# A squared-ReLU MLP in seven products per pair: feature pairs worked on two at a time, and operand reloads issued ahead and split over the products

## The chip, the cores and the metric

The kernel runs on one core of a Trainium2 chip. The metric is the device time of one execution in microseconds (us); the median of the runs is compared.

## What is computed

One layer of a diffusion backbone over 1024 tokens of width 1024, in fp32. The part around the change is the MLP at its end:

```python
def sq_relu_mlp(h, w1, w2):
    return jnp.square(jax.nn.relu(h @ w1.astype(jnp.float32))) @ w2.astype(jnp.float32)
...
hm = modulate(rmsnorm(xs_, pre_mlp_g[i]), sh2, sc2)
xs_ = xs_ + g2 * rmsnorm(sq_relu_mlp(hm, w_mlp1[i], w_mlp2[i]), post_mlp_g[i])
```

`h` is 1024 x 1024, `w1` is 1024 x 4096, `w2` is 4096 x 1024.

## The kernel before

Each matmul operand is held as two fp32r parts, a high half (a copy on ACT) and a low half (a difference on DVE). A product of two such operands takes three matmuls for each 128 rows of the contraction.

Both layers of the MLP are computed with a Strassen-Winograd scheme: a 2 x 2 block product in seven block products instead of eight. A "pair" is two feature tiles of 128, one from either half, and both token blocks of 512. For each pair there are seven products, in the order 1, 2, 6, 5, 7, 3, 4 (`ORDER`, line 1155). A product (`mm_op`, line 1217) is 12 matmuls of 128 x 128 by 128 x 512. Three PSUM banks hold the seven: bank x takes products 1, 6, 7 and 4 one upon the other, bank y takes 5 and 3, bank v takes 2. Between two products on a bank, `evac` reads the bank: in layer one with a copy (`snap`, on ACT) or a sum (on DVE) into `stage`, then ReLU and square on ACT; in layer two into `acc`, copies on ACT for the first chunk and sums on DVE after it.

There are 27 pairs. Layer one has 13 in this form (`S1`), after three done as plain products; each ends with four sums (`finish`) and a write of `stage` to `hid_d` in DRAM, from the POOL queue. Layer two has 14 (`S2`): four chunks of the hidden features, four pairs each, less two that the final stage does as plain products. `s_pair` (line 1225) runs a pair: after each product it evacuates, takes one step of the generator `wgen`, which prepares one of the next pair's seven weight operands (`wop`: a copy and a difference, and four sums a pair), and calls `beside`.

The weights of a pair are two loads of 512 KB (`wload`, lines 1158 to 1166) from the SP queue. There is room for two pairs: the first half in the pool of `raw`, the second in `raw2`, two buffers each. Seven buffers hold the weight operands, so one is prepared as soon as the same product of the pair before has been done.

The seven operands made of tokens (`hop`) are ready in layer one. In layer two each chunk has its own seven. `refill` (line 1351) and `load_op` (line 1356) bring one: four loads of 256 KB from `hid_d` into the four buffers `sq` (named `hraw` when they hold a load; the snaps use the same four), each followed by a copy on ACT and a difference on DVE. Each operand has one buffer, so it is refilled after its product in the last pair of a chunk: line 1373 for the change of layers, line 1401 for the changes of chunk (`o == 3`).

`stage` has two buffers, which hold `xr` before layer one and `acc` after it. At the start three of the operands are still to be split: 6 and 7 from one half of `xr`, 4 from the other (lines 1303 to 1310). Operand 4 goes into the buffer in which `stg` was written out.

The program gives the order in which instructions are wished for. A planner sets each engine's actual order when the kernel is built, by its own estimate of durations; on the chip each engine then follows its order and waits on semaphores.

Of the kernel before, what the change touches and what calls it, by code (L numbers as in the profile page):

```python
# [8 lines left out]
F32 = mybir.dt.float32  # L9
# [6 lines left out]
P = 128  # L16
KT = 8
# [26 lines left out]
def hybrid_block(ctx, tc, A):  # L44
# [39 lines left out]
    def tt(out, a, b, op, eng=ve):  # L84
        eng.tensor_tensor(out=out, in0=a, in1=b, op=op)  # L85
# [1070 lines left out]
    BLK = {1: 0, 2: 1, 3: 2, 5: 3, 6: 4, 7: 5, 4: 6}  # L1156

    def wload(src):
        if wraw:
            r1 = wp.tile([P, KT, P], F32, tag="raw", name="raw")  # L1160
        else:
            r1 = wx.tile([P, KT, P], F32, tag="raw2", name="raw2", bufs=2)
        sy.dma_start(r1, src[0])
        r2 = wx.tile([P, KT, P], F32, tag="raw2", name="raw2", bufs=2)
        sy.dma_start(r2, src[1])
        return r1, r2

    def wsplit(i, src):
# [7 lines left out]
    def wgen(raw, out):  # L1176
        r1, r2 = raw
        a11, a12, a21, a22 = r1[:, 0:4], r1[:, 4:8], r2[:, 0:4], r2[:, 4:8]
        s2 = t3.tile([P, 4, P], F32, tag="s2", name="s2")
        tt(a21, a11, a21, ALU.subtract)  # L1180
        tt(s2, a22, a21, ALU.subtract)
        out[1] = wsplit(0, a11)
        yield
        tt(a11, a11, s2, ALU.add)
        out[2] = wsplit(1, a12)
        yield
        tt(a12, a12, s2, ALU.subtract)
        out[6] = wsplit(2, s2)
        yield
        out[5] = wsplit(3, a11)  # L1190
        yield
        out[7] = wsplit(4, a21)
        yield
        out[3] = wsplit(5, a12)
        yield
        out[4] = wsplit(6, a22)
# [6 lines left out]
    wraw, wops, at = [], [], [0]  # L1203

    def wraw_upto(n):
        while len(wraw) < min(n, len(srcs)):
            wraw.append(wload(srcs[len(wraw)]))

    def next_gen():
        i = len(wops)  # L1210
        if i == len(srcs):
            return None
        wraw_upto(i + 1)
        wops.append({})
        return wgen(wraw[i], wops[i])

    def mm_op(ps, w, h, start):
        for k in range(4):
# [3 lines left out]
            pe.matmul(ps, a, s, start=False, stop=False, skip_group_check=not start)  # L1222
            pe.matmul(ps, b_, r, start=False, stop=k == 3, skip_group_check=not start)  # L1223

    def s_pair(w, ops, evac, beside):
        x = dense_ps("sx")
        yw = pair_ps("syw")
        y, v = yw[:, 0], yw[:, 1]
        bank = {1: x, 6: x, 7: x, 4: x, 5: y, 3: y, 2: v}
        gen = next_gen()  # L1230
        for p in ORDER:
            mm_op(bank[p], w[p], ops[p], p in (1, 5, 2))
            evac(p, bank[p])
            step_(gen)
            beside(p)
            if p == 1:
                wraw_upto(len(wops) + 1)


    def mm_plain(w, b):  # L1240
# [26 lines left out]
    h0, h1 = xr  # L1267
    lo4, hi4 = slice(0, 4), slice(4, 8)
    wraw_upto(1)
    gen0 = next_gen()  # L1270
    step_(gen0)

    def hm_sums():
        tt(h0[:, lo4], h1[:, lo4], h0[:, lo4], ALU.subtract)
# [18 lines left out]
    for p in range(3):  # L1293
        for i in range(2):
            ps = mm_plain(next_piece(), 1)
            step_(hs)
            relu2(stg[:, (7, 0)[i]], ps)
        if p == 1:
            step_(gen0, 2)
        t_sums(hd[:, 2 * p], stg[:, 7], hd[:, 2 * p + 1], stg[:, 0], stg[:, 1:5])  # L1300
        gp.dma_start(hid_d[0][:, 2:7, p], stg[:, 0:5])
    hops = {1: hop[0, 0], 2: hop[0, 1], 3: hop[1, 1], 5: hop5}
    hops[6] = z_op("b")
    split_op(hops[6], h1[:, hi4])
    step_(gen0, 4)
    wraw_upto(2)
    hops[7] = z_op("a")
    split_op(hops[7], h1[:, lo4])
    hops[4] = z_op("c")
    split_op(hops[4], h0[:, hi4])  # L1310

    late = [None]

    def hidden(c, j):
        st = poolB.tile([P, KT, TB], F32, tag="B", name="stage")
        keep = {}

        def snap(ps):
            t = t3.tile([P, TB], F32, tag="sq", name="snap", bufs=4)
            act(t, ps, AF.Copy)  # L1320
            return t

        def sq(k):
            act(st[:, k], st[:, k], AF.Relu)
            act(st[:, k], st[:, k], AF.Square)

        def evac(p, ps):
            if p in (1, 6, 5):
                keep[p] = snap(ps)
# [19 lines left out]
    slots = {}  # L1349

    def refill(c, p):
        o = a_op() if p in (1, 2, 5, 3) else z_op({6: "b", 7: "a", 4: "c"}[p])
        load_op(o, c, BLK[p])
        slots[p] = o

    def load_op(o, c, blk):
# [6 lines left out]
    done = None  # L1363
    for i, (c, j) in enumerate(S1):
        evac, finish = hidden(c, j)
        prev_done = done
        last = i == len(S1) - 1

        def beside(p):
            if p == 1 and prev_done:  # L1370
                prev_done()
            if last and p not in (3, 4):
                refill(0, p)

        s_pair(wops[i], hops, evac, beside)
        done = finish
    done()
    refill(0, 3)
    refill(0, 4)


    acc = [poolB.tile([P, KT, TB], F32, tag="B", name=f"acc{b}") for b in range(NB)]
# [4 lines left out]
        else:  # L1387
            tt(t, t, ps, ALU.add)

    for i, (c, o) in enumerate(S2):  # L1390
# [6 lines left out]
        ops = dict(slots)  # L1397

        def beside(p):
            if o == 3:  # L1400
                refill(c + 1, p)

        s_pair(wops[len(S1) + i], ops, evac, beside)
    esX.close()


# [138 lines left out]
```

## Time and profile before

| | us |
|---|---|
| median of 3 runs | 1465.84 (1465.63 to 1467.81) |
| the profiled execution | 1462.37 |
| its span, first to last instruction | 1460.6 |
| mean granted TensorE clock, share of full speed | 0.987 |
| TensorE busy | 1406.6 (96%) |
| DVE busy | 1037.8 (71%) |
| ACT busy | 736.8 (50%) |

TensorE is the engine to look at. A busy share is a mean over stages; the stages are to be looked at one by one, and in each the question is what ended TensorE's idle time. An operation is named by what it writes and what it reads (`hop<-hraw`: an operand from a load), by engine and by line; L85 and L88 are the helpers for sums on DVE and copies on ACT, L1221 to L1223 the three matmuls of `mm_op`. The banks are named sx (x) and syw (y and v).

### The profile page before, as it was taken

What the parts mean: (1) busy time and instruction counts of PE and PEld (TensorE: products, weight loads), DVE (VectorE), ACT (ScalarE), POOL (GpSimd) and SP (SyncE); (2) the same over time, 40 slices, a digit from 0 to 9 for tenths busy, and PEclk for the clock granted to TensorE, in tenths of its full rate; (3) what the DMA queues carried; (4) which work ended last, traced back from release to release, by engine and by line L of the source; (5) the groups of instructions that cost most, each with busy time, mean ns of one, the idle gap of its engine ahead of it and who ended that gap; (6) DMA issues with size and microseconds to landing.
All of it is one profiled execution on the core that took longest, in us unless ns stands there. A gap on an engine that the chain in (4) does not pass through costs nothing. (4 is left out here: it accounts for less than half of the span.)

```text
span 1460.6 us, 18131 instructions
## 1 busy us (share of the span) xinstructions
PE 1406.6 (96%) x6760; PEld 1094.6 (75%) x6760; DVE 1037.8 (71%) x1604; ACT 736.8 (50%) x1148; POOL 45.1 (3%) x92
## 2 busy tenths in 40 slices
PE   6999899999999999999999989999997999999996
PEld 2667778788887588878757768888876787878775
DVE  2699599887776698654686776666666577787726
ACT  4876655555553721242365555555556363434534
POOL 0000100000000000000000000000000000000000
PEclk8999999999999999999999999999999999999998
DMA  9411634432224232678534434444457364444533
GB/s 388 165 54 57 157 108 148 147 100 84 82 78 142 79 108 109 206 269 312 177 116 159 137 121 170 142 150 153 166 204 248 95 191 126 149 147 130 174 123 115
DMA packets 77049, 218.60 MB, mean 150 GB/s; under 512 B 8865, under 2 KB 15137, under 8 KB 74530
## 3 DMA queue, kind: packets, MB, share of 16 engines
q1 hardware_dynamic: 67058, 186.25, 38.5%
q0 software_dynamic: 9904, 31.20, 5.8%
q8 instruction: 53, 0.87, 0.2%
q14 instruction: 34, 0.28, 0.1%
HBM read 164.07 MB, written 53.35 MB: 149 GB/s over the span
## 5 line engine op out<-in xcount | busy, mean ns | idle before, releaser
L1221 PE MATMUL sx<-hop,wop 128*128 128x512 f32 x432 | 172.3, 399 | 12.8 <-ACT snap L88 5.7
L172 PE MATMUL dn<-h_hi,whi 128*128 128x512 f32 x448 | 179.4, 400 | 1.1 <-ACT Cf L88 1.1
L175 PE MATMUL dn<-h_hi,wlo 128*128 128x512 f32 x448 | 177.3, 397 | 0.0
L174 PE MATMUL dn<-h_lo,whi 128*128 128x512 f32 x448 | 177.2, 396 | 0.0
L88 ACT ACTIVATE wop<-raw 128x512 fp32r<-128x512 f32 x162 | 101.3, 627 | 142.7 <-PE syw L1223 69.8
L1222 PE MATMUL sx<-hop,wop 128*128 128x512 f32 x432 | 172.0, 398 | 0.0
L1223 PE MATMUL sx<-hop,wop 128*128 128x512 f32 x432 | 170.1, 396 | 0.0
L85 DVE TENSOR_TENSOR wop<-raw,wop 128x512 fp32r<-128x512 f32 x162 | 111.4, 689 | 51.0 <-ACT wop L88 50.3
L88 ACT ACTIVATE whi<-raw 128x1024 fp32r<-128x1024 f32 (+1 forms) x76 | 78.6, 1034 | 127.8 <-PE mixp L174 56.4
L85 DVE TENSOR_TENSOR wlo<-raw,whi 128x1024 fp32r<-128x1024 f32 (+1 forms) x76 | 90.6, 1193 | 64.7 <-ACT whi L88 64.2
L1221 PE MATMUL syw<-hop,wop 128*128 128x512 f32 x324 | 128.5, 397 | 4.3 <-ACT snap L88 3.6
L1222 PE MATMUL syw<-hop,wop 128*128 128x512 f32 x324 | 128.2, 396 | 0.0
L1223 PE MATMUL syw<-hop,wop 128*128 128x512 f32 x324 | 126.8, 392 | 0.0
L1221 PEld LDWEIGHTS sx<-hop,wop 128*128 128x128 f32 x432 | 82.3, 191 | 35.2 <-ACT snap L88 6.9
L172 PEld LDWEIGHTS dn<-h_hi,whi 128*128 128x128 f32 x448 | 84.2, 188 | 24.6 <-issue 7.5
L174 PEld LDWEIGHTS dn<-h_lo,whi 128*128 128x128 f32 x448 | 84.2, 188 | 22.1 <-issue 6.0
L175 PEld LDWEIGHTS dn<-h_hi,wlo 128*128 128x128 f32 x448 | 84.2, 188 | 20.4 <-issue 3.8
L88 ACT ACTIVATE hop<-hraw 128x512 fp32r<-128x512 f32 x116 | 70.7, 626 | 51.5 <-DMA hraw<-hid_d 50.9
L1223 PEld LDWEIGHTS sx<-hop,wop 128*128 128x128 f32 x432 | 82.4, 191 | 18.7
L1222 PEld LDWEIGHTS sx<-hop,wop 128*128 128x128 f32 x432 | 82.2, 190 | 18.7 <-DVE hop L85 0.8
L85 DVE TENSOR_TENSOR hop<-hraw,hop 128x512 fp32r<-128x512 f32 x116 | 76.9, 686 | 19.1 <-ACT hop L88 18.5
L1221 PEld LDWEIGHTS syw<-hop,wop 128*128 128x128 f32 x324 | 61.2, 189 | 21.2 <-ACT snap L88 4.2
(313 smaller groups left out, 2833.7 us busy)
## 6 DMA issues: line engine op xcount, KB each, us to landing
raw<-in_w_mlp SPq DMA_DIRECT2D x70, 512.0 KB, 3.6
hraw<-hid_d SPq DMA_DIRECT2D x116, 256.0 KB, 3.1
raw<-in_w_in SPq DMA_DIRECT2D x38, 512.0 KB, 3.8
hid_d<-stage POOLq DMA_DIRECT2D x9, 1792.0 KB, 7.6
wa<-in_w_ada SPq DMA_DIRECT2D x24, 512.0 KB, 4.5
raw<-in_w_out SPq DMA_DIRECT2D x22, 512.0 KB, 3.9
wada<-in_w_ada SPq DMA_DIRECT2D x8, 1024.0 KB, 9.9
E<-rows_d SPq DMA_DIRECT2D x32, 256.0 KB, 4.4
```

The costliest lines, as they stand in the source:

```text
L85: eng.tensor_tensor(out=out, in0=a, in1=b, op=op)
L88: return ac.activation(out=out, in_=in_, func=f, bias=bias, scale=scale)
L172: ins = pe.matmul(out, a, r, start=start and k == 0, stop=False)
L174: pe.matmul(out, a, s, start=False, stop=False)
L175: last_mm[0] = pe.matmul(out, b, r, start=False, stop=stop and k == kn - 1)
L1221: pe.matmul(ps, a, r, start=start and k == 0, stop=False, skip_group_check=not start)
L1222: pe.matmul(ps, a, s, start=False, stop=False, skip_group_check=not start)
L1223: pe.matmul(ps, b_, r, start=False, stop=k == 3, skip_group_check=not start)
```

## The change

- The pairs are put in groups: (0, 1), then 2 to 10 one by one, then (11, 12), (13, 14) and so on in twos through layer two. `s_group` runs a group product by product: product 1 of the first pair, product 1 of the second, product 2 of the first, and so on. Each pair has its own banks x, y and v.
- The weight operands are prepared in that order too, still seven ahead. Both halves of an even pair are loaded into `raw2`, both of an odd one into `raw`; a pair's load is placed after the last weight operand of the pair two before it.
- In layer one the snaps of products 6 and 5, and mostly that of product 1, are written into `stage` directly.
- The refill of a chunk's operands begins in the last group (two pairs) of the chunk before. A slot's four loads are issued when the slot is free and the one before it is converted; the conversion is done one or two pieces per product (`convert`).
- At the start the remaining plain weights are all requested a step earlier, pair 1's weights behind them; operand 4 is placed ahead of operand 7. In the final stage the last operand (`b12`) is loaded ahead of the first step.

The diff, cut to this:

```diff
     def wload(src):
-        if wraw:
-            r1 = wp.tile([P, KT, P], F32, tag="raw", name="raw")
-        else:
-            r1 = wx.tile([P, KT, P], F32, tag="raw2", name="raw2", bufs=2)
-        sy.dma_start(r1, src[0])
-        r2 = wx.tile([P, KT, P], F32, tag="raw2", name="raw2", bufs=2)
-        sy.dma_start(r2, src[1])
-        return r1, r2
+        rs = []
+        for i in range(2):
+            if len(wraw) % 2:
+                rs.append(wp.tile([P, KT, P], F32, tag="raw", name="raw"))
+            else:
+                rs.append(wx.tile([P, KT, P], F32, tag="raw2", name="raw2", bufs=2))
+            sy.dma_start(rs[i], src[i])
+        return rs
...
+    groups = [(0, 1)] + [(i,) for i in range(2, 11)] + [(i, i + 1) for i in range(11, len(srcs), 2)]
+    seq = [(i, p) for gr in groups for p in ORDER for i in gr]
...
+    def next_op():
+        if at[0] == len(seq):
+            return
+        i, p = seq[at[0]]
+        at[0] += 1
+        if p == 1:
+            wraw_upto(i + 1)
+            wops[i] = {}
+            wg[i] = wgen(i)
+        next(wg[i], None)
+        if p == 4:
+            wraw_upto(i + 3)
...
-    def s_pair(w, ops, evac, beside):
-        x = dense_ps("sx")
-        yw = pair_ps("syw")
-        y, v = yw[:, 0], yw[:, 1]
-        bank = {1: x, 6: x, 7: x, 4: x, 5: y, 3: y, 2: v}
-        gen = next_gen()
+    def s_group(gr, ops, evacs, beside):
+        bank = {}
+        for i in gr:
+            x = dense_ps("sx")
+            yw = pair_ps("syw")
+            y, v = yw[:, 0], yw[:, 1]
+            bank[i] = {1: x, 6: x, 7: x, 4: x, 5: y, 3: y, 2: v}
         for p in ORDER:
-            mm_op(bank[p], w[p], ops[p], p in (1, 5, 2))
-            evac(p, bank[p])
-            step_(gen)
-            beside(p)
-            if p == 1:
-                wraw_upto(len(wops) + 1)
+            for i, evac in zip(gr, evacs):
+                mm_op(bank[i][p], wops[i].pop(p), ops[p], p in (1, 5, 2))
+                evac(p, bank[i][p])
+                next_op()
+                beside(p, i == gr[-1])
...
         if p == 1:
-            step_(gen0, 2)
+            fetch(len(order))
+            wraw_upto(2)
+            for _ in range(2):
+                next_op()
...
-    step_(gen0, 4)
-    wraw_upto(2)
+    next_op()
+    next_op()
+    hops[4] = z_op("c")
+    split_op(hops[4], h0[:, hi4])
     hops[7] = z_op("a")
     split_op(hops[7], h1[:, lo4])
-    hops[4] = z_op("c")
-    split_op(hops[4], h0[:, hi4])
-
-    late = [None]
-
-    def hidden(c, j):
+    next_op()
+    next_op()
+
+    def hidden(c, j, apart):
...
-        def snap(ps):
-            t = t3.tile([P, TB], F32, tag="sq", name="snap", bufs=4)
+        def snap(p, ps):
+            if p == 1 and apart:
+                t = t3.tile([P, TB], F32, tag="sq", name="snap", bufs=4)
+            else:
+                t = st[:, {1: 0, 6: 7, 5: 2}[p]]
             act(t, ps, AF.Copy)
             return t
...
+    def op_pieces(o, c, blk):
         for k in range(4):
             s = t3.tile([P, TB], F32, tag="sq", name="hraw", bufs=4)
             sy.dma_start(s, hid_d[c][:, blk, k])
+            queue.append((o, k, s))
+
+    def convert(n):
+        for o, k, s in queue[:n]:
             act(o[:, 0, k], s, AF.Copy)
             tt(o[:, 1, k], s, o[:, 0, k].bitcast(F32), ALU.subtract)
+        del queue[:n]
+
+    class Refill:
...
+        def __call__(self, p, freed):
+            if queue:
+                convert(2 if self.n % 2 == 0 else 1)
+                self.n += 1
+            if self.todo and freed:
+                self.ready.append(p)
+                self.fresh.discard(p)
+                self.todo -= 1
+            if self.ready and not queue:
+                p = self.ready.pop(0)
+                o = a_op() if p in (1, 2, 5, 3) else z_op({6: "b", 7: "a", 4: "c"}[p])
+                op_pieces(o, self.c, BLK[p])
+                slots[p] = o
+                self.fresh.add(p)
...
+        if gr[-1] == len(S1) - 1:
+            refill.start(0)
+
+        def beside(p, last):
+            if first:
+                first.pop(0)()
+            if p == 4 and len(ends) == 2:
+                ends.pop(0)()
+            refill(p, last)
...
+        c, o = S2[gr[0] - len(S1)]
+        if o == 2:
+            refill.start(c + 1)
+        s_group(gr, Slots(), [adder(*S2[i - len(S1)]) for i in gr], refill)
...
-    step(parts[0], 2)
-    load_op(b12, 3, 7)
+    op_pieces(b12, 3, 7)
+    step(parts[0], 1)
+    convert(2)
+    step(parts[0], 1)
+    convert(2)
     step(parts[0], 2)
```

## Rows read from the trace of the kernel before

**Rows 1.** The page: its span, and section 1's row of busy time.
```profile
span 1460.6 us, 18131 instructions
PE 1406.6 (96%) x6760; PEld 1094.6 (75%) x6760; DVE 1037.8 (71%) x1604; ACT 736.8 (50%) x1148; POOL 45.1 (3%) x92
```

**Rows 2.** Windows by stage: busy us (x instructions) of each engine, clock, DMA.
```profile
core 0: us, PE busy (x) PEld busy (x) DVE busy (x) ACT busy (x) POOL busy (x), PEclk, DMA share, GB/s
844.92:888.45 43.53, 38.57 (x157) 30.12 (x156) 30.88 (x42) 24.26 (x38) 1.84 (x2) 0.96 0.40 139
888.45:1081.72 193.27, 193.27 (x842) 157.67 (x840) 118.82 (x181) 106.86 (x180) 9.52 (x10) 1.00 0.43 153
1081.72:1174.94 93.22, 83.48 (x337) 66.56 (x336) 58.43 (x92) 44.91 (x80) 1.70 (x2) 0.93 0.54 180
1174.94:1392.25 217.31, 214.96 (x925) 172.58 (x924) 170.77 (x268) 101.27 (x170) 0.00 (x0) 1.00 0.51 163
```

**Rows 3.** Timeline of PE: start and duration (us) of matmuls where products begin.
```profile
805.47 0.39 PE L1221 MATMUL syw<-hop,wop 128*128 128x512 f32 x1
...
844.92 0.39 PE L1221 MATMUL sx<-hop,wop 128*128 128x512 f32 x1
...
1081.72 0.39 PE L1221 MATMUL sx<-hop,wop 128*128 128x512 f32 x1
```

**Rows 4.** Waits of PE, 840 to 1400 us: total us, times, longest.
```profile
PE sx L1221 <- ACT snap L88: 5.7, 3, 4.4
PE sx L1221 <- ACT acc L88: 5.4, 2, 3.7
PE syw L1221 <- ACT snap L88: 3.6, 1, 3.6
PE sx L1221 <- DVE acc L85: 1.6, 2, 1.4
```

**Rows 5.** Chain of waits at the change of layers: start us, us, what.
```profile
1090.04 7.24 DMA hraw<-hid_d
...
1098.97 0.49 ACT snap L88
...
1122.77 8.05 DMA hraw<-hid_d
...
1133.08 0.49 ACT acc L88
```

**Rows 6.** Chain of waits at the start of layer one.
```profile
852.21 9.44 DMA hid_d<-stg
...
861.67 0.03 ACT hop L88
...
864.62 0.49 ACT snap L88
```

**Rows 7.** Windows, the product behind the 4.4 us wait (columns as in rows 2).
```profile
1099.50:1105.00 5.50, 5.49 (x13) 4.33 (x14) 1.65 (x3) 1.00 (x2) 0.00 (x0) 0.50 0.46 143
```

**Rows 8.** Groups, 1174.9 to 1216 us (busy, mean ns), then DVE's timeline, two in a row.
```profile
L85 DVE TENSOR_TENSOR hop<-hraw,hop 128x512 fp32r<-128x512 f32 x28 | 18.7, 686 | 2.1 <-ACT hop L88 1.9
...
1122.06 1.28 DVE L85 TENSOR_TENSOR hop<-hraw,hop 128x512 fp32r<-128x512 f32 x2
```

**Rows 9.** DMA issues of the page (KB, us to landing), then landing times of raw.
```profile
hraw<-hid_d SPq DMA_DIRECT2D x116, 256.0 KB, 3.1
...
hid_d<-stage POOLq DMA_DIRECT2D x4, 2048.0 KB, 9.7
...
DMA to landing us min/median/max: 3.4/3.5/7.2
```

**Rows 10.** Line 1345, the stage writes: timeline of two issues, and landing times.
```profile
1084.65 0.84 POOL L1345 DMA_DIRECT2D hid_d<-stage  x1 [18.48 <-DVE stage L85]
...
1120.80 0.85 POOL L1345 DMA_DIRECT2D hid_d<-stage  x1 [35.30 <-ACT hop L88]
...
DMA to landing us min/median/max: 7.1/7.7/12.6
```

More of the change, by code (lines that the diff above doesn't have):

```diff
@@ L1158, in wload, with wsplit @@
     def wload(src):
-        if wraw:
-            r1 = wp.tile([P, KT, P], F32, tag="raw", name="raw")
-        else:
-            r1 = wx.tile([P, KT, P], F32, tag="raw2", name="raw2", bufs=2)
-        sy.dma_start(r1, src[0])
-        r2 = wx.tile([P, KT, P], F32, tag="raw2", name="raw2", bufs=2)
-        sy.dma_start(r2, src[1])
-        return r1, r2
-    def wsplit(i, src):
+        rs = []
[6 more added lines that the diff above has]
+        return rs
+    nsplit = [0]
+    def wsplit(src):
+        i = nsplit[0] % 7
+        nsplit[0] += 1
         if i < 3:
@@ L1174, in wsplit, with wgen @@
         return o
-    def wgen(raw, out):
-        r1, r2 = raw
+    def wgen(i):
+        r1, r2 = wraw[i]
+        out = wops[i]
         a11, a12, a21, a22 = r1[:, 0:4], r1[:, 4:8], r2[:, 0:4], r2[:, 4:8]
-        s2 = t3.tile([P, 4, P], F32, tag="s2", name="s2")
+        out[1] = wsplit(a11)
         tt(a21, a11, a21, ALU.subtract)
+        s2 = t3.tile([P, 4, P], F32, tag=("s2", "rs_r")[i % 2], name="s2")
         tt(s2, a22, a21, ALU.subtract)
-        out[1] = wsplit(0, a11)
         yield
         tt(a11, a11, s2, ALU.add)
-        out[2] = wsplit(1, a12)
+        out[2] = wsplit(a12)
         yield
         tt(a12, a12, s2, ALU.subtract)
-        out[6] = wsplit(2, s2)
+        out[6] = wsplit(s2)
         yield
-        out[5] = wsplit(3, a11)
+        out[5] = wsplit(a11)
         yield
-        out[7] = wsplit(4, a21)
+        out[7] = wsplit(a21)
         yield
-        out[3] = wsplit(5, a12)
+        out[3] = wsplit(a12)
         yield
-        out[4] = wsplit(6, a22)
+        out[4] = wsplit(a22)
         yield
@@ L1202, in hybrid_block @@
     srcs += [(A["w_mlp2"][c, o], A["w_mlp2"][c, o + 4]) for c, o in S2]
-    wraw, wops, at = [], [], [0]
+    groups = [(0, 1)] + [(i,) for i in range(2, 11)] + [(i, i + 1) for i in range(11, len(srcs), 2)]
+    seq = [(i, p) for gr in groups for p in ORDER for i in gr]
+    wraw, wops, wg, at = [], {}, {}, [0]
     def wraw_upto(n):
@@ L1207, in wraw_upto @@
             wraw.append(wload(srcs[len(wraw)]))
[L1209 to L1215, printed above, removed]
+    def next_op():
[10 more added lines that the diff above has]
+            wraw_upto(i + 3)
     def mm_op(ps, w, h, start):
@@ L1304, in hybrid_block @@
     split_op(hops[6], h1[:, hi4])
-    step_(gen0, 4)
-    wraw_upto(2)
+    next_op()
+    next_op()
+    hops[4] = z_op("c")
+    split_op(hops[4], h0[:, hi4])
     hops[7] = z_op("a")
     split_op(hops[7], h1[:, lo4])
-    hops[4] = z_op("c")
-    split_op(hops[4], h0[:, hi4])
-    late = [None]
-    def hidden(c, j):
+    next_op()
+    next_op()
+    def hidden(c, j, apart):
         st = poolB.tile([P, KT, TB], F32, tag="B", name="stage")
         keep = {}
-        def snap(ps):
-            t = t3.tile([P, TB], F32, tag="sq", name="snap", bufs=4)
+        def snap(p, ps):
[3 more added lines that the diff above has]
+                t = st[:, {1: 0, 6: 7, 5: 2}[p]]
             act(t, ps, AF.Copy)
@@ L1328, in evac @@
             if p in (1, 6, 5):
-                keep[p] = snap(ps)
+                keep[p] = snap(p, ps)
             elif p == 2:
@@ L1347, in hidden @@
         return evac, finish
[L1349 to L1356, printed above, removed]
+    slots, queue = {}, []
+    def op_pieces(o, c, blk):
         for k in range(4):
@@ L1359, in load_op, with __init__, start @@
             sy.dma_start(s, hid_d[c][:, blk, k])
+            queue.append((o, k, s))
+    def convert(n):
+        for o, k, s in queue[:n]:
             act(o[:, 0, k], s, AF.Copy)
             tt(o[:, 1, k], s, o[:, 0, k].bitcast(F32), ALU.subtract)
[L1363 to L1379, printed above, removed]
+        del queue[:n]
+    class Refill:
+        def __init__(self):
+            self.ready, self.n, self.todo, self.fresh = [], 0, 0, set()
+        def start(self, c):
+            assert not (self.ready or queue or self.todo)
+            self.c, self.todo = c, 7
+        def __call__(self, p, freed):
[12 more added lines that the diff above has]
+                self.fresh.add(p)
+    refill = Refill()
+    done = []
+    for gr in groups:
+        if gr[0] >= len(S1):
+            break
+        hid = [hidden(*S1[i], i == 0 or len(gr) == 2 and i == gr[1]) for i in gr]
+        first, ends = list(done), [h[1] for h in hid]
+        done = ends
+        if gr[-1] == len(S1) - 1:
[6 more added lines that the diff above has]
+            refill(p, last)
+        s_group(gr, hops, [h[0] for h in hid], beside)
+    for d in done:
+        d()
     acc = [poolB.tile([P, KT, TB], F32, tag="B", name=f"acc{b}") for b in range(NB)]
@@ L1388, in add_up, with adder @@
             tt(t, t, ps, ALU.add)
-    for i, (c, o) in enumerate(S2):
+    def adder(c, o):
         a11, a12, a21, a22 = (acc[b][:, m] for m in (o, o + 4) for b in range(NB))
@@ L1395, in evac, with __getitem__ @@
             add_up(t, ps, c == 0 and p in (1, 6, 5, 4))
[L1397 to L1403, printed above, removed]
+        return evac
+    class Slots:
+        def __getitem__(self, p):
+            assert p in refill.fresh and not any(slots[p] is q[0] for q in queue)
+            return slots[p]
+    for gr in groups:
+        if gr[0] < len(S1):
+            continue
+        c, o = S2[gr[0] - len(S1)]
+        if o == 2:
+            refill.start(c + 1)
+        s_group(gr, Slots(), [adder(*S2[i - len(S1)]) for i in gr], refill)
     esX.close()
```

2 lines of the change are left out of this document (removed).

## The prediction

> **What bounds the kernel now.** I read the page's header first: TensorE is busy 1406.6 of 1460.6 us [rows 1], so only time in which it stands, or runs at its lower clock, can be won. Then the windows by stage, cut where the timeline shows a pair of the MLP begin [rows 2, 3]. The undisturbed rate is the second window: ten pairs in 193.27 us at clock 1.00, 19.33 us a pair and 2.761 us a product (12 matmuls). All 27 pairs of the stage at that rate would take 521.9 us. Against that rate:
> - Start, 844.92 to 888.45: 43.53 us for two pairs, of which one product ran early, at 805.47 [rows 3]. Due: 38.65 - 2.76 = 35.89. Lost: 7.6 us.
> - Layer one to layer two, 1081.72 to 1174.94: 93.22 us for four pairs (due 77.31). Lost: 15.9 us.
> - Rest of layer two, 1174.94 to 1392.25: 217.31 us for eleven pairs (due 212.60), three changes of chunk in it. Lost: 4.7 us.
>
> Together 28.2 us. This is all that the change can win in the stage.
>
> What ends those waits is read from the table of waits: TensorE stood for ACT's copies out of a bank (snap, acc) and DVE's sums (acc), at most 4.4 us at once [rows 4]. The engines were not short of work: the copies were late because their engine stood. The chain of waits shows it: at 1090.04 a reload (hraw) takes 7.24 us to land, ACT's next operand half waits for it, and the snap comes behind it; at 1122.77 it is 8.05 us, with acc behind [rows 5]. At the start it is the write of stg to hid_d, 9.44 us, with an operand half, and then snap, behind it [rows 6]. After the 4.4 us wait the clock was 0.50 for the whole next product, 13 matmuls in 5.5 us instead of 3.0 [rows 7]: a long wait costs 2.5 us more than itself.
>
> **The change, part by part.**
>
> *Two pairs, product by product.* Bank x takes products 1, 6, 7, 4 in turn, each after the copy of the one before. With one pair, one other product lies between (2.76 us of cover); with two, three do (8.28 us). An evacuation that today makes TensorE wait 4.4 us is 2.76 + 4.4 = 7.2 us late, still inside 8.28. So each wait of [rows 4] would vanish if lateness stayed as it is. The number of instructions on the three engines stays the same: the snaps that now go straight into stage are the same copies. Pairs 2 to 10 stay single and lose nothing now; cost and gain 0 there.
>
> *Reloads spread.* A refill is 28 pieces: a load, a copy on ACT and a difference on DVE each, 0.686 us on DVE alone, about 0.61 in a row [rows 8]. Today they crowd into one pair; now one or two follow each product. By the code's counting a slot takes three products, so the seven are ready 4, 7, 10, 13, 16, 19, 22 products after the group's first, and are read at 14, 16, 18, 20, 22, 24, 26: 4 products (11 us) to spare at the tightest, against a landing of 3.1 us at the median [rows 9]. DVE's load in such a group: 18 instructions a pair (181 for ten pairs, 0.656 us each [rows 2]) and some 18.7 pieces, so 36 x 0.656 + 18.7 x 0.61 to 0.686 = 35.0 to 36.4 us of 38.65. It fits, with little over. The three chunk changes: 4.7 us now, left 0 to 4.7; I take 0.5, since evacuation has 8.28 us of cover.
>
> *The change of layers.* Here a new wait appears. acc uses the buffers of the last two stages, 11 and 12, which are now written out together. A write is issued 2.9 us after its pair ends (1084.65 against 1081.72 [rows 3, 10]) and a 2 MB write lands in 9.7 us at the median and 12.6 at most [rows 9, 10]. With S the end of layer one, pair 11 ends at S - 2.76, its write lands between S + 9.9 and S + 12.8, and product 1's copy into acc is done 0.6 us later. TensorE wants that bank for product 6 at S + 4 x 2.76 = S + 11.0: a wait of 0 to 2.4 us. If the two writes share the engines evenly, the first lands near S + 16.8: a wait of 6.4 us and 2.5 for the clock. Behind the copy on ACT are queued weight halves and operand halves; these have 6 and 4 products of lead. The second write lands by S + 19.6 to 25, and the bank behind it is wanted at S + 22.1: 0 to 3. Bounds 0 to 10; I take 4, near the 12.6 us row, which is a 2 MB write beside reloads, as here.
>
> What the rings do with two writes is also stated by the Trainium skill (DMA: Bandwidth & Descriptors, section "Queues, rings and completion order"): one ring is consumed in order, and different rings take turns. By that rule the first write is not slowed by the second, and the wait is the 0 to 2.4 us; by even sharing it is 6.4 us. The trace has no two stage writes at once; that reloads slow down beside one (8.05 us beside the write issued at 1120.80, median 3.1) agrees with the turns.
>
> Group (11, 12) has a smaller new wait of the kind: stage 12 needs the buffer of stage 10, whose write is issued 2.9 us into the group and lands 9.7 to 12.6 us later, at 12.6 to 15.5; product 2 of pair 12 asks for it on DVE at 11.0. DVE may stand 1.6 to 4.5 us, with weight differences behind it; 8.28 us of cover hides that. Cost 0; without the cover, 4.5.
>
> *The start.* Products 1 and 2 of both pairs need only operands that are ready early, so TensorE has up to 11 us of work where it now has less. Against it: pair 1's weights and seven more halves fall into the busiest stretch of ACT and DVE, and pair 1's stage needs the second half of xr, which is free once the last operand is split. That split waits for the write that landed at 852.21 + 9.44 = 861.65 [rows 6] and is through some 4 us later, at 866 to 868; product 7 of pair 1 wants a copy into that stage by 844.92 + 9 x 2.76 - 2.76 = 867.0. Left: 0 to today's 7.6 and 2.5 more if a long wait lowers the clock; I take 3.
>
> *Loads moved.* Weight pairs now come in pairs of the same kind of buffer, and SP issues those of a group's successor behind the reloads. The last split of pair i is placed after product 6 of a group's 14, the second half of the raw load for pair i+2 goes out some 2 us later, and its first use is two products (5.5 us) after that split. A load lands in 3.5 us at the median, 7.2 at most [rows 9]: DVE stands 0 to 3.7 us, hidden by the 8.28. Cost 0; without that cover up to 3.7 us at each of eight entries. The final stage's b12 reload is issued earlier, before its first step; TensorE there does not wait for it now. Cost 0, within 1 us either way.
>
> **Sum.** Lost now 28.2; left 3 + 4 + 0.5 = 7.5; gain 20.7 us. The profiled execution took 1462.4 us (span 1460.6 and 1.8 around it) and would take 1441.7. The median of the runs is 1465.84, 3.4 us above that execution, so I predict 1465.84 - 20.7 = 1445.1 us, 1445.
>
> **Rivals.**
> - *Everything is absorbed.* The first write is alone in its ring and the start fits: 1.5 us left, 1439. For it: all present lateness is under 8.28 us. Against it: even one write lands up to 1.8 us after the bank is wanted, and there are two. Chance 0.15. The ring order that the Trainium skill states (DMA: Bandwidth & Descriptors, the section above) would lead here or close to it.
> - *The stage writes become the bound.* They share, reloads beside them slow down, the start stays as it is: 10 + 7.6 + 2 = 19.6 left, gain 8.6, 1457. For it: 8.05 us reloads beside a single write. Against it: the reloads are issued products ahead. Chance 0.13.
> - *Late weights, slower.* At the eight entries into a new group (pair 2 and the seven groups of layer two) ACT's split and DVE's first difference stand before a raw load that could not be issued earlier, and the copies stand behind them. TensorE loses from the point where a 512 KB load takes more than 3.5 + 8.28 = about 12 us. If each entry then costs 4 us of standing and 2.5 of clock, 8 x 6.5 = 52 us stand against the 28.2 won: 1465.84 + 52 - 28.2 = 1490. It is slower from 3.5 us an entry. For it: a single write took 12.6 us under reloads. Against it: no raw load of the stage took over 7.2. Chance 0.09. The Trainium skill's rule that buffers be doubled (Trainium Kernel Development and Optimization, section "Best Practices") speaks for this rival, as both sets of raw buffers belong to the group at work; the trace cannot show it, as today a whole pair is loaded ahead.
> - *It does not do what it says.* Each engine's order is fixed when the kernel is built; if the copies are again placed behind reloads that land late, and by more than the new cover, the waits return: gain under 3 us, 1465. The early product at 805.47 shows that the order is not that of the code. Chance 0.05.
>
> **How the numbers follow.** Forecast 0.58 (1440 to 1453), rivals 0.15, 0.13, 0.09, 0.05. The range goes from 1437 (nothing left, 28.2 won) to 1459, which takes in most of the second rival and leaves out about 0.17. A measurement tells some 0.2% (2.9 us) from no change: faster 0.86, same 0.05, slower 0.09.
>
> **What would show it.** In the changed kernel the single pairs 2 to 10 still take 19.33 us each; a refilling group in layer two takes 38.65 to 39.5; no TensorE wait on a copy over 1 us is left at the three chunk changes; at the change of layers one wait on acc of 1 to 6 us ends with the landing of a stage write; at the start at most one wait over 2 us. Wrong if waits on wop appear at the entries of groups (late weights), if DVE is busy over 95% of a refilling group with TensorE waiting for it, or if the loss at the change of layers stays above 10 us.

## The result, and the profile after

The changed kernel takes 1453.24 us (median of 10 runs, 1451.03 to 1457.18) beside 1465.74 us of the kernel before on the same chip (10 runs). The ratio is 0.9916, with a 95% interval of 0.9896 to 0.9936: 12.5 us faster, where 20.7 were forecast. The time is inside the range, the sign is right, and the gain is six tenths of the forecast one.

The page of the profiled execution after (1451.86 us, to stand beside 1462.37 us before), which answers [rows 1]:

```profile
span 1450.1 us, 18140 instructions
PE 1402.3 (97%) x6760; PEld 1095.9 (76%) x6760; DVE 1034.3 (71%) x1604; ACT 734.0 (51%) x1148; POOL 45.2 (3%) x92
```

TensorE executes the same 6760 matmuls; what changes is the time in which it stands or runs slowly. The stage of the 27 pairs now goes from 847.67 to 1381.77 us. The windows of after by stage, with the columns of [rows 2]: the hole before the stage, the first group, pair 2 and its neighbours, more single pairs, the change of layers, the rest of layer two.

```profile
800.18:847.67 47.49, 43.73 (x179) 34.94 (x178) 39.02 (x39) 28.54 (x38) 2.49 (x3) 0.93 0.41 139
847.67:887.73 40.06, 40.06 (x176) 32.66 (x175) 30.84 (x43) 25.61 (x42) 0.87 (x1) 1.00 0.33 116
887.73:947.84 60.11, 55.83 (x236) 45.24 (x235) 32.84 (x51) 29.03 (x50) 3.91 (x4) 0.97 0.49 175
947.84:1076.78 128.94, 128.94 (x561) 105.11 (x560) 79.40 (x122) 72.17 (x123) 6.59 (x7) 1.00 0.45 159
1076.78:1167.82 91.04, 86.68 (x371) 70.33 (x370) 64.72 (x104) 53.43 (x97) 1.70 (x2) 0.98 0.61 202
1167.82:1381.77 213.95, 213.95 (x932) 174.55 (x930) 167.83 (x264) 92.20 (x155) 0.00 (x0) 1.00 0.54 171
```

How to read a loss out of such a row: take its length and subtract its matmuls times 0.2301 us, the undisturbed rate (193.27 us for ten pairs of 84 matmuls, [rows 2]). Third row: 60.11 - 236 x 0.2301 = 5.8 us lost. Fifth: 91.04 - 371 x 0.2301 = 5.7. Second, fourth and sixth: nothing. (A matmul that a cut counts twice is 0.2 us, so this is good to about half a us.) The kernel before lost 7.6 at the start, 15.9 at the change of layers and 4.7 after it; of these only the second remains, smaller, and a new loss stands at pair 2. The table of waits, to be held against [rows 4], has two rows left for the whole stage:

```profile
PE sx L1233 <- ACT acc L88: 4.4, 1, 4.4
PE sx L1233 <- ACT stage L88: 4.3, 1, 4.3
```

**Pair 2.** The chain of waits of after before that wait (start us, us, what):

```profile
888.59 10.08 DMA hid_d<-stage
...
898.75 0.60 ACT stage L88
...
899.40 0.77 PE sx L1233
```

ACT's copy of pair 2's product 1 goes straight into pair 2's stage tile. That tile's buffer is the one from which stage 0 is still being written out; the write was issued at 888.59 and lands 10.1 us later, and TensorE can accumulate product 6 into the bank only after the copy. Product 1 of pair 3 was already run ahead in this gap, at 891.93, so the wait would have been longer without it.

**Change of layers.** Layer one ends at 1104.96. The stage writes of POOL (start, us, then the idle time before), and the end of the chain of waits:

```profile
1107.47 0.85 POOL L1362 DMA_DIRECT2D hid_d<-stage  x1 [37.39 <-DVE stage L85]
1113.22 0.85 POOL L1362 DMA_DIRECT2D hid_d<-stage  x1 [4.90 <-issue]
```

```profile
1107.85 3.06 DMA hraw<-hid_d
...
1112.06 6.86 DMA hraw<-hid_d
...
1119.48 0.61 ACT wop L88
1120.10 0.49 ACT acc L88
...
1120.63 0.50 PE sx L1233
```

Stage 11's write lands 10.9 us after its issue, at 1118.4; a reload piece lands at 1118.92. (This piece was requested 4.6 us behind the write and took 6.86 us; the one requested 0.4 us behind it took 3.06.) ACT stands for the piece, and behind it come a weight half and the copy into acc, for which TensorE waits. Both causes end within 0.6 us of each other, so the trace alone doesn't say which counts. The experiments say more.

The clock after each of these two waits, in windows (PEclk is the third column from the right):

```profile
899.40:903.09 3.69, 3.69 (x9) 2.97 (x10) 1.27 (x2) 1.73 (x3) 0.00 (x0) 0.54 0.64 258
1120.63:1124.99 4.36, 4.36 (x12) 3.46 (x13) 3.45 (x6) 2.38 (x5) 0.00 (x0) 0.61 1.00 380
```

Nine matmuls in 3.69 us where 2.07 are due, twelve in 4.36 where 2.76 are: each wait costs 1.6 us more than itself; the same kind of row cost 2.5 us before [rows 7].

**The hole before the stage.** In [rows 3] one product of pair 0 ran at 805.47. After, TensorE's timeline has nothing there:

```profile
807.66 0.39 PE L175 MATMUL m<-hop,wlo 128*128 128x512 f32 x1
810.88 0.80 PE L172 MATMUL m<-hop,whi 128*128 128x512 f32 x1 [2.83 <-ACT whi L88]
```

The product now runs inside the stage, which makes that 2.76 us longer.

**The sum.** The stage's losses fall from 28.2 to 12.2 us (6.0 at pair 2, 6.2 at the change of layers, measured matmul by matmul): 16.0 won. The product that is no longer early takes 2.8 back: the stage lasts 534.1 us instead of 547.3. It begins 2.75 us later than in the trace of before; 2.4 of that stands already before the hole, where the last plain matmul begins at 805.23 before and at 807.66 after, and the stage's start lies between 846.1 and 850.2 in the kernels below, so I put no cause to it. 13.2 - 2.75 is the 10.5 us between the two spans. The tail behind the stage is unchanged (68.33 and 68.35 us).

### The profile page after: what moved, and what is told of

Same layout as the page of the kernel before. It is cut to its first block, busy times and chain, and to the rows that moved or that the text cites. A ratio compares the mean times of both kernels' runs of the same rounds, so it can differ in the third digit from the quotient of the medians.

```text
span 1450.1 us, 18140 instructions
## 1 busy us (share of the span) xinstructions
PE 1402.3 (97%) x6760; PEld 1095.9 (76%) x6760; DVE 1034.3 (71%) x1604; ACT 734.0 (51%) x1148; POOL 45.2 (3%) x92
## 5 line engine op out<-in xcount | busy, mean ns | idle before, releaser
L85 DVE TENSOR_TENSOR hop<-hraw,hop 128x512 fp32r<-128x512 f32 x116 | 77.1, 685 | 15.7 <-ACT hop L88 15.4
## 6 DMA issues: line engine op xcount, KB each, us to landing
wada<-in_w_ada SPq DMA_DIRECT2D x8, 1024.0 KB, 10.5
```

## The experiments

Each kernel starts from the changed one unless said otherwise. This table gives the losses in us, worked out from windows as above (before: the hole in its own window, shown with the last experiments, the rest from [rows 2]), and the time: the median for the kernels given with an interval, one execution for the others.

| kernel | hole | first group | pair 2 | change of layers | rest | us |
|---|---|---|---|---|---|---|
| before | 3.3 | 7.4 | 0 | 15.7 | 4.5 | 1465.7 |
| after | 6.3 | 0 | 5.8 | 5.7 | 0 | 1453.2 |
| snap_pair2 | 6.4 | 0 | 7.4 | 7.0 | 0 | 1457.2 |
| split_write | 6.7 | 0 | 7.2 | 8.4 | 0 | 1455.4 |
| short_writes | 6.0 | 0 | 0.4 | 0.4 | 0 | 1441.4 |
| burst | 5.8 | 0 | 7.5 | 11.5 | 0.4 | 1459.1 |
| single_all | 3.2 | 3.6 | 0 | 14.7 | 8.2 | 1464.0 |
| single01 | 1.6 | 4.0 | 0 | 7.2 | 0 | 1447.6 |
| early | 1.6 | 1.0 | 3.9 | 6.3 | 0 | 1449.8 |
| end_first_early | 1.6 | 0.9 | 0 | 5.3 | 0 | 1444.3 |
| tail_single | 3.2 | 1.3 | 0 | 4.3 | 0 | 1443.2 |
| rolling | 1.4 | 0.9 | 0 | 4.0 | 0 | 1442.0 |

(split_write was timed too: ratio 0.9925, 0.9892 to 0.9958.) Between kernels that are the same at a place, the loss there differs by 1 to 2 us (pair 2 in after and burst, the change of layers in after, early and single01); smaller differences are not read.

### What pair 2 waits for

**snap_pair2** takes the three copies of pair 2 out of the stage tile:

```diff
-            if p == 1 and apart:
+            if p in own and apart:
```
(own is (1, 6, 5) for pair 2, and (1,) elsewhere)

> The changed kernel, but pair 2's three snaps go into the sq buffers, as in the kernel before, and not into stage. Theory (the copy of pair 2's product 1 waits for the stage buffer, which pair 0's late write holds; the edit that lets snaps go into stage made this wait): pair 2's wait of 4.3 us and the slow product behind it are gone, 27 pairs in 528 us; the 6.1 us at the change of layers stay. Rival (DVE stood 3.9 us behind the raw load that landed at 895.3, and that holds the evacuations): pair 2 still loses 3 us or more, on a later product, 531 to 534 us.

It took 1457.17 us; the 27 pairs took 536.8 us, more than either side expected. The table of waits of snap_pair2:

```profile
PE syw L1233 <- DVE stage L85: 4.5, 1, 4.5
PE sx L1233 <- ACT acc L88: 4.5, 1, 4.5
```

The expectation missed. The wait at pair 2 didn't go, it moved to the next instruction that writes into the same tile: DVE's sum of products 1 and 2. That sum starts at 901.66, when the same write, issued at 891.13, has landed (10.51 us). So the copy is not what is late; the buffer is, but the edit couldn't prove that.

**split_write** writes five or six of a stage's blocks after product 3 and the rest at the end:

```diff
+                gp.dma_start(hid_d[c][:, 0, j], st[:, 0])
+                gp.dma_start(hid_d[c][:, 2:6, j], st[:, 2:6])
```
(behind product 3's sums; blocks 1 and 6 follow at the end)

> The changed kernel, but each stage of layer one is written to hid_d in two parts: what is final after product 3 (five or six of the blocks) at once, and the two blocks that need product 4 behind it. Same sums, same bytes. The MLP's 27 pairs took 534.1 us in the changed kernel, 12.2 over the undisturbed 521.9: 6.1 in pair 2 and 6.1 at the change of layers, each a wait of 4.3 to 4.4 us and a product at the lower clock. Theory (the writes of a group's two stages go out together, late, and the next owner of the buffer waits for them): both waits are gone, the 27 pairs take 522 to 525 us, the execution 1440 to 1445. Rival (ACT and DVE stand behind loads, raw in pair 2 and hraw at the change of layers; the writes only happen to land then): the loads are the same, both waits stay at 3 us or more, 530 to 534 us, the execution 1450 to 1455.

It took 1455.42 us (1452.64 to 1457.77), the 27 pairs 537.9 us. That is outside both ranges and nearer the rival's. POOL's timeline and the chain of waits of split_write:

```profile
884.52 0.76 POOL L1360 DMA_DIRECT2D hid_d<-stage  x1 [16.01 <-issue]
...
889.34 0.54 POOL L1369 DMA_DIRECT2D hid_d<-stage  x1 [0.32 <-DVE stage L85]
```

```profile
889.34 7.80 DMA hid_d<-stage
...
897.32 0.61 ACT stage L88
```

The first part leaves 4 us earlier, the last 256 KB leave at 889.34, no earlier than the whole did, and take 7.80 us behind the rest. Counted from the stage's start the buffer comes free 1.2 us sooner, which the scatter swallows. Writing the same bytes in parts doesn't help where the last block is the late one.

**short_writes** makes the write itself small:

```diff
+            if i in (0, 11):
+                n = 1
             gp.dma_start(hid_d[c][:, 0:n, j], st[:, 0:n])
```
(the blocks left out are filled with other pairs' data from stages 3, 5, 7 and 9)

> Stages 0 and 11 write one of their 7 or 8 blocks (256 KB instead of 1.75 and 2 MB) at their end; the other blocks of hid_d in these two places are filled with other pairs' data, out of stages 3, 5, 7 and 9, so that part of the computation is left out. Theory (TensorE's two waits are for buffers that a stage write still reads): pair 2's loss falls from 6.0 to under 1 us, and the loss at the change of layers from 6.2 to under 2; the 27 pairs take 522 to 526 us, in all 1441 to 1445. Rival (at the change of layers the reloads of the operands set the end, whatever stage 11 writes): pair 2's loss goes, that at the change of layers stays at 4 to 6; 526 to 529 us, in all 1446 to 1449. Second rival (pair 2 waits for its raw weights, which made DVE stand 3.9 us there): 3 us or more of pair 2's loss stay.

It took 1441.36 us, and the 27 pairs took 523.3 us against 521.9 undisturbed. Its windows at pair 2 and at the change of layers:

```profile
887.92:947.94 60.02, 59.45 (x259) 48.16 (x257) 36.98 (x58) 32.52 (x56) 3.73 (x4) 1.00 0.47 167
...
1077.02:1168.09 91.07, 90.86 (x394) 73.61 (x393) 69.74 (x111) 55.79 (x101) 0.86 (x1) 1.00 0.61 203
```

60.02 - 259 x 0.2301 = 0.4 and 91.07 - 394 x 0.2301 = 0.4. Both losses go, though pair 2's raw loads and the reloads are the same and stage 12 is still written in full. The theory holds at both places: the writes of stages 0 and 11 set them. Stage 12's write alone beside the reloads, of which one still took 7.6 us, cost next to nothing. What this run can't tell is whether, at the change of layers, stage 11's write counts as the holder of acc's buffer or as a burden on the reloads beside it. That is end_first_early's question.

### Cover, or reloads issued ahead

**burst** keeps the pairs in twos but loads and converts a whole operand at once:

```diff
-            if queue:
-                convert(2 if self.n % 2 == 0 else 1)
-                self.n += 1
...
                 op_pieces(o, self.c, BLK[p])
+                convert(4)
```

> The changed kernel, but a slot's four loads and its four conversions are placed together as soon as the slot is free, as in the kernel before; pairs are still worked on in twos. Theory (three products of cover for each evacuation are what took the waits away, the spread is not needed for it): the three changes of chunk lose under 2 us together, the change of layers 4 to 9, 27 pairs in 532 to 537 us. Rival (the spread is what did it; in a burst ACT stands behind each slot's loads): the changes of chunk lose 4 us or more together and the change of layers 12 or more, 27 pairs in 543 us or more.

It took 1459.08 us, the 27 pairs 542.4. The window of burst at the change of layers, and its chain of waits there:

```profile
1075.53:1166.64 91.11, 80.78 (x346) 65.48 (x345) 60.78 (x98) 49.62 (x90) 1.70 (x2) 0.94 0.55 185
```

```profile
1095.56 4.02 DMA hraw<-hid_d
...
1110.61 4.00 DMA hraw<-hid_d
...
1115.92 10.31 DMA hid_d<-stage
...
1126.32 0.61 ACT acc L88
```

91.11 - 346 x 0.2301 = 11.5, twice that of after, and the 27 pairs come close to the rival's 543. The pieces themselves land in 4 us. The harm is indirect: the conversions stand in ACT's and DVE's queues until their pieces land, the sums of stage 11 come behind them, and its write is issued at 1115.92 instead of 1107.47. At the three chunk changes, where no stage is written, the bunched reloads cost 0.4, as the theory had it: each side was right at one place.

**single_all** does the opposite: reloads issued one product ahead of their conversions, no pairs in twos.

```diff
-    groups = [(0, 1)] + [(i,) for i in range(2, 11)] + ...
+    groups = [(i,) for i in range(len(srcs))]
```
(and all four pieces of an operand are converted after the next product; a chunk's refill begins in its last pair)

> No two pairs are worked on together anywhere; the reloads stay issued ahead, all four loads of a slot after one product and its four conversions after the next. Theory (the second pair in between covers late copies): without it the waits of the kernel before come back in part, 3 to 5 us at the start, 8 us or more at the change of layers, 2 to 5 us at the three chunk changes: 27 pairs in 535 to 540 us, in all 1450 to 1456. Rival (issuing ahead is what won the time in layer two): change of layers 6 us or less, chunk changes under 1; 27 pairs in 529 to 533, in all 1445 to 1449.

It took 1463.98 us beside 1463.89 of the kernel before: no gain. Its windows at the change of layers and after it:

```profile
1076.23:1167.13 90.90, 79.77 (x331) 63.07 (x329) 57.25 (x90) 45.95 (x82) 1.70 (x2) 0.96 0.54 174
1167.13:1393.89 226.76, 221.72 (x950) 178.45 (x948) 173.07 (x271) 98.30 (x165) 0.00 (x0) 0.99 0.51 161
```

14.7 and 8.2 us lost, 22.9 together, where before lost 15.7 and 4.5 by the same reckoning. The theory's side is right, but the 27 pairs took 546.8 us, more than its 535 to 540. So the cover by a second pair is what wins the chunk changes (burst, with the cover and without the spread, loses 0.4 there), and without it this way of asking one product ahead wins nothing. At the change of layers, cover alone (burst) still loses 11.5 and both together 5.7.

**single01** takes the first group apart and leaves the others:

```diff
-    groups = [(0, 1)] + [(i,) for i in range(2, 11)] + ...
+    groups = [(i,) for i in range(11)] + ...
```

> The changed kernel, but pairs 0 and 1 are worked on one after the other; pairs 11 to 26 stay in twos, and the order of the operand splits and loads at the start stays as changed. Theory (working in twos is what took away the 7.6 us of the start, and also what delays the two writes on which pair 2 waits): the start loses 5 to 9 us again, pair 2 nothing, 27 pairs in 533 to 537 us. Rival (the start's gain came from placing operand 4 ahead of operand 7 and from the earlier requests): the start loses under 2 us, pair 2 nothing, 528 us.

It took 1447.59 us, faster than after; the 27 pairs, one product of which ran early again (at 808.30), took 531.0 us. The start loses 4.0 us, between the two expectations, and pair 2 nothing: putting pairs 0 and 1 together wins 4.0 and costs 5.8 at pair 2. Against before (7.4) the start gains 3.4 without any pair in twos; which of the moved loads and operands does that I didn't separate.

### The early product, and the first pair brought to its end

**early** prepares the operand of pair 0's second product second instead of third:

```diff
+    seq[1], seq[2] = seq[2], seq[1]
```
(and calls next_op twice, not once, ahead of the norm's sums)

> The second weight operand that is prepared is again the one of pair 0's second product, so that one product of 12 matmuls can again stand in the hole before 817 us. Theory (the changed order of operand preparation emptied the hole): the time that TensorE loses between 800 us and the stage's start falls from 6.5 to about 3.7 us (12 matmuls, 2.8 us), the 27 pairs lose 12 us as before (waits at pair 2's product 6 and at the change of layers unchanged), 1450.5 us. Rival (the hole is set by the norm's own copies and differences, and the added operand only delays them): still 6 us or more are lost there, 1453 us.

It took 1449.84 us. The same window of before and of early (two kernels, one fence each):

```profile
800.02:844.92 44.90, 43.36 (x181) 34.84 (x180) 34.81 (x33) 27.77 (x36) 2.48 (x3) 0.96 0.41 140
```

```profile
800.46:847.87 47.41, 45.87 (x199) 37.10 (x198) 38.81 (x39) 30.23 (x40) 2.59 (x4) 1.00 0.49 159
```

47.41 - 199 x 0.2301 = 1.6 lost instead of 6.3; the product runs at 810.03 again and the clock stays at 1.00 over the window (0.93 in after). More than the 2.8 expected, by the clock. Pair 2 still loses 3.9 and the change of layers 6.3, as the theory said.

**end_first_early** adds the repair that short_writes points to, with all data written. The groups of layer one alternate for four products only:

```diff
+        if len(gr) == 2 and gr[0] < len(S1):
+            a, b = gr
+            head = [(i, p) for p in ORDER[:4] for i in gr]
+            return head + [(a, p) for p in ORDER[4:]] + [(b, p) for p in ORDER[4:]]
```

> The two groups of layer one (pairs 0 and 1, pairs 11 and 12) alternate for the first four products of each pair only; then the first pair runs to its end, and the second after it, so that the first pair ends two products (5.5 us) sooner. The operand of pair 0's second product is prepared second, as in the run early. Theory (stage writes set both waits, 4.3 and 4.4 us): both fall under 1 us, no wait over 1 us comes at the start; the loss of the 27 pairs falls from 12.2 to 0 to 4 us, and that before the stage by 2.8; in all 1453.2 - 10 - 2.8 = 1440, within 1438 to 1444. Rival (the reload that lands within half a us of stage 11's write at the change of layers sets the end): 4 to 6 us stay there, 1444 to 1447. Second rival (four products in turn are not enough at the start, product 7 of pair 0 waits for its operand): 2 to 4 us come back there.

1444.31 us (1444.08 to 1444.43), ratio 0.9862 (0.9845 to 0.9878): 1.4% under before, and below the interval of after. Pair 2's wait is gone, as is the wait on ACT's acc. But the change of layers still loses 5.3 us, 4.2 of it by two waits of 2.0 on DVE's acc. The window, and the chain of waits behind them:

```profile
1077.35:1168.44 91.09, 86.68 (x373) 69.26 (x371) 64.47 (x104) 51.95 (x94) 1.70 (x2) 1.00 0.60 203
```

```profile
1097.25 7.96 DMA hraw<-hid_d
...
1113.05 7.54 DMA hraw<-hid_d
...
1126.18 6.50 DMA raw<-in_w_mlp
...
1136.11 0.61 DVE acc L85
...
1136.76 0.50 PE sx L1242
```

The stage writes were issued at 1095.67 and 1110.99; the loads requested 1.6 and 2.1 us after them took 8.0 and 7.5 us instead of 3.1 [rows 9]. The first wait ends behind a reload beside stage 12's write. The second ends behind a load of weights: requested at 1126.18, 4.4 us after that write had landed, it took 6.50 us, and DVE stood 5.6 us for it. So the reading is that stage 11's write counted twice: as the holder of acc's buffer (gone with the earlier end), and as a burden on the reloads, which the chain carries on to the weights. The first half is shown, most plainly in burst, where the copy into acc begins as that write lands; the second is argued from the chain and from short_writes, where stage 12's write alone cost next to nothing. Theory for pair 2, rival's number for the change of layers.

**tail_single** takes the second group of layer one apart as well, so that stage 11 is written some 13 us earlier than in end_first_early, counted from the stage's start:

```diff
-    groups = [(0, 1)] + [(i,) for i in range(2, 11)] + [(i, i + 1) for i in range(11, len(srcs), 2)]
+    groups = [(0, 1)] + [(i,) for i in range(2, 13)] + [(i, i + 1) for i in range(13, len(srcs), 2)]
```

> As end_first_early, but pairs 11 and 12 are worked on one after the other (pair 11 is written out 19 us before layer one ends), and the reloads for layer two's first group, which now begin a whole pair later, are converted two pieces per product instead of one or two. Theory (at the change of layers TensorE waits because stage 11's write both holds a buffer that acc needs and slows the reloads issued beside it): the loss there falls from 5.5 to 0 to 2.5 us, as in the run that wrote only an eighth of stage 11; 1444.3 - 4 = 1440, within 1438 to 1442. Rival (any 2 MB write beside the reloads slows them enough: stage 12's does it too, and single pairs have one product of cover where pairs in twos have three): 5 to 12 us are lost there, 1444 to 1451.

1443.17 us (1441.23 to 1445.29), ratio 0.9839 (0.9822 to 0.9856), which overlaps that of end_first_early. The change of layers loses 4.3 instead of 5.3, a difference within the scatter. POOL's issue and the chain of waits of tail_single:

```profile
1080.29 0.84 POOL L1371 DMA_DIRECT2D hid_d<-stage  x1 [18.48 <-DVE stage L85]
```

```profile
1082.82 7.41 DMA hraw<-hid_d
...
1090.26 0.63 ACT hop L88
1090.88 0.50 ACT stage L88
```

The collision has moved with the write: the refill now begins beside it, a piece takes 7.41 us, ACT stands for it, and pair 12, single, has one product of cover. The loss lies between the two expectations, nearer the rival's.

**rolling** asks for every piece two products ahead of its conversion:

```diff
+            if s is None or q[5] > now - 2:
+                break
```
(in convert; a piece is requested as soon as one of the four buffers is free)

> As tail_single, but a reload's four pieces are requested one by one as their buffers come free, and each is converted two products (5.5 us) or more after its request instead of one (2.8 us). Theory (what is left at the change of layers in tail_single, 4.6 us, is ACT standing 4.9 us for a piece requested at 1082.82 that took 7.4 us beside stage 11's write): most of it is now covered by the longer lead, 0.5 to 2.5 us are left there, in all 1443.2 - 3 = 1440, within 1438 to 1442. Rival (the pieces land later the earlier they are requested, since the write is the same and shares the engines with them): 4 us or more stay there, 1443 or more.

1441.99 us (1438.21 to 1444.52), ratio 0.9821 (0.9795 to 0.9847). The chain of waits, ACT's timeline and the table of waits of rolling:

```profile
1083.89 6.98 DMA hraw<-hid_d
```

```profile
1085.09 1.30 ACT L88 ACTIVATE stage<-stage 128x512 f32<-128x512 f32 x2
1090.89 0.63 ACT L88 ACTIVATE hop<-hraw 128x512 fp32r<-128x512 f32 x1 [4.50 <-DMA hraw<-hid_d]
```

```profile
PE sx L1242 <- ACT stage L88: 2.3, 1, 2.3
```

The loss stays at 4.0, where 0.5 to 2.5 were expected; that is the rival's number, but it doesn't show the rival's cause, since the piece that counts got no longer lead. It was requested 2.5 us behind stage 11's write (1083.89 against 1081.36), as in tail_single (1082.82 against 1080.29), and ACT was free for it 2.5 us after the request (at 1086.39), again as in tail_single (at 1085.33). Whether a real lead of two products would help stays open. The last three kernels can't be told from each other by their times; all three are faster than before and than the change as it was made.

## Why the prediction came out as it did

- **What can be won.** Right: only TensorE's losses changed, and none of the engines beside it became the bound (DVE 167.83 of 213.95 us in the rest of layer two).
- **Chunk changes.** Forecast 0.5 left, found 0. Right, by the mechanism named: single_all, without the cover, loses 8.2 there, and burst, with it, 0.4.
- **The start.** Forecast 3 left, found 0. Mis-sized on the safe side; the late split of pair 1's stage, which I feared, made no wait of TensorE.
- **Pairs 2 to 10: "cost and gain 0 there".** This step failed; the truth is 6.0 us, all at pair 2. My own working had the question that was needed. For stage 12 I counted the time from the issue of stage 10's write to the first use of its buffer; for pair 2, which takes stage 0's buffer, I didn't. By the same terms stage 0's pair ends at 883.6, its write is issued 2.9 us later and lands 9.7 to 12.6 behind that, at 896.2 to 899.1; the copy of 0.6 us then ends at 896.8 to 899.7, and TensorE had no other work from 894.96 on: 1.8 to 4.7 us, and the clock. These are the terms of a 2 MB write; stage 0's has 1.75 MB, and with the 7.7 us median of all writes [rows 10] no wait would have come out. In the trace both terms are longer: the write is issued 5.0 us after its pair's end and takes 10.08. A single pair before had the whole pair in between, 19.33 us; a pair that follows a group of two has one product.
- **Change of layers.** Forecast 4 left, found 6.2. The mechanism is right as far as it goes (one wait on acc, 4.4 us, behind the landing of stage 11's write); the term mis-sized is the issue of the write, 5.2 us after its pair's end (1107.47 against 1102.23) instead of 2.9, because in a group the sums of one pair stand behind the evacuations of the other. The copy began 1.7 us after the write had landed, behind the reload piece and a weight half: that reloads beside the write land as late as the write itself I had put aside as covered by 4 to 6 products of lead.
- **The ring order** that the Trainium skill states (DMA: Bandwidth & Descriptors, section "Queues, rings and completion order") agrees with the trace in one point: stage 1's write, issued 1.2 us behind stage 0's, landed 4.2 us behind it (after 13.1 us, the other after 10.1), where even sharing would let the two end about as far apart as they began. That the first was not slowed at all isn't shown: the lone writes of its size before took 7.1 to 8.8 us, and here two loads of weights ran beside it as well. The 1439 us to which the rule seemed to lead didn't come, since pair 2 lost 6.0 us and the write at the change of layers was issued later than the forecast had it.
- **The early product.** I used the row at 805.47 as proof that the engines' order isn't that of the code, and didn't ask whether the change leaves its operand in time. It doesn't, which costs 2.8 us, and early wins them back.
- **Loads moved.** DVE stood 3.9 us for pair 2's raw load, which had landed by 895.29; the copy for which TensorE waits began at 898.75, when stage 0's write had landed. Hidden, as said, so the rival of late weights is out for the change as it was made. In end_first_early a late load of weights is behind one wait of 2.0 us.

Together: 6.0 at pair 2, 2.2 more at the change of layers and 2.8 for the early product, less 3.0 at the start and 0.5 at the chunk changes, make 7.5 us, which is the forecast 20.7 less the 13.2 by which the stage became shorter. That the time still fell well inside the range is in part luck: 11.0 us of misses one way were met by 3.5 the other way.

## What to carry to other kernels

Working on two units in turn gives each copy more cover, but it also brings the two ends together, so that the buffers of both come free late and the next unit finds none: for each buffer, count from the issue of its last reader to its next writer, for the unit after the group too. Alternate only as long as the cover is needed, then bring the first unit to its end; that removed the wait at pair 2, while at the change of layers other waits took its place. And before an operand is moved in the order of preparation, look in the trace for work that ran early because that operand was there.

## What the runs showed of the hardware

- Loads of 256 KB requested 0.5 to 5.2 us behind the write of a stage on another queue took 6.9 to 10.2 us in after, where 3.1 is the median before [rows 9]; five in before, end_first_early, tail_single and rolling, requested 1.6 to 2.5 us behind a write, took 7.0 to 8.1. One requested 0.4 us behind a write took 3.06 (after).
- Two stage writes issued 1.2 us apart on one queue landed 4.0 to 4.4 us apart (after, snap_pair2, burst).
- After waits of 4.28 and 4.36 us the granted clock was 0.54 and 0.61 for the next 3.7 and 4.4 us, which is the 1.2 GHz level for most of them; after one of 2.75 us (tail_single) it was 0.62 for 4.4 us, after one of 2.32 (rolling) it was 1.00. In end_first_early, whose longest wait there is 2.0 us, the clock stayed at 1.00 over the whole change of layers. Two waits of 2.0 cost 4.2 us in all, one of 4.4 costs 6.
